# Second mixers off GpSimd, later transposes, reordered norm steps, and wider weight splits in a two-block transformer kernel

## The chip, the cores and the metric

The kernel runs on one core of a Trainium2 chip. The metric is device time of one execution, in microseconds (us). Three runs of the kernel before took 2176.16, 2175.93 and 2166.27 us, median 2175.93 us.

TensorE does matmuls and transposes, VectorE (DVE), ScalarE (ACT) and GpSimd (POOL) do the elementwise work, and SyncE (SP) issues the loads.

## The reference

The input is one sequence of 256 tokens of width 1024, float32. It goes through two layers of a first block and two of a second. Feed-forward layers have width 2816.

```python
for l in range(DEPTH):          # first block
    x = layer_norm(ALPHA * x + 0.5 * swiglu(x, ffn1_w13[l], ffn1_w2[l]), ln_g[l, 0], ln_b[l, 0])
    m = mixer(x, w_in[l], ...)  # gated recurrence (hgrn2), spatial gating unit, two branches
    x = layer_norm(ALPHA * x + m, ln_g[l, 1], ln_b[l, 1])
    x = layer_norm(ALPHA * x + 0.5 * swiglu(x, ffn2_w13[l], ffn2_w2[l]), ln_g[l, 2], ln_b[l, 2])
...
# second block, per layer: a feed-forward layer, token_mixer, a feed-forward layer,
# each between two rms_norms and added to x
qk = lax.conv_general_dilated(qk, conv_w, ...)   # in token_mixer: a filter of 5 taps along the tokens
qk = jax.nn.silu(qk + conv_b)
h_fwd = mlstm_direction(mq, mk, mv, gates[0], gates[1])   # and one backwards
merged = jnp.concatenate([attn_out, mlstm_out], axis=-1)
return merged @ w_out
```

## The kernel before

**Units and splits.** The weights come in units of 128 x 1024 floats. To keep precision, each operand is split into a high part (`hi`, written by ScalarE as a rounded copy) and a low part (`lo = w - hi`), and `mm3` does three matmuls: `x_hi w_hi`, `x_hi w_lo`, `x_lo w_hi`. In traces the parts of a weight unit are `wh` and `wl`, those of the transposed input of a layer `xh` and `xl`, those of hidden values `hT`. `split` does a unit's split. A plain unit comes from one of 4 staging buffers (`stg`) and is split in two halves of 512 columns, so that the second half's copy runs beside the first half's subtraction. `pool_share` gives every third second half of units 8 to 27 of a second mixer to GpSimd (L272).

**Products.** In the feed-forward layers some pairs of groups of columns are computed with seven products of sums of blocks in place of eight (`PRODUCTS`, `pair`). Their weight operands are blocks loaded raw (`raw`) and sums of them, which `operand` adds up on VectorE just ahead of that unit's split; a product unit is split at full width, 1024.

**Order.** The two halves of the tokens (128 each, i = 0 and 1) are two generators. Each `yield` ends a unit of TensorE work and moves a clock by one; `yield n` lets a generator or a side chain pause n clocks; `self.later(n, fn)` writes the instructions of `fn` n clocks later. From what is so written a scheduler makes the order of TensorE, VectorE and ScalarE; GpSimd and SyncE keep the written order. Each engine executes its instructions in order, so an instruction that waits holds all behind it.

**Places that the change touches.** `hidden` (L435, and the one in `pair`) finishes gate times value (`sg` L442/L445, `kp` L511) and leaves the transposes to `turn`, 2 clocks later. `ln_residual` is the first block's norm: per half h of the columns it makes `t` (L583) and its statistics, then `u` (named `t`, L592) and `x` (L593); `to_x` transposes the two `x` and writes `xh` and `xl` (L311). `sgu` is the spatial gating unit (its normed `v`, L862). In a second mixer `gates` (L1072 on) turns the gate columns `m` (L1000) with TensorE (L1080), and makes `gg`, `gc`, `Gh`, `Gl` for `mlstm`. `conv` filters `cv` into `qk`: three of four parts on VectorE, the fourth on GpSimd (L1128, L1136, L1137), and waits for it before it goes on. `rot` turns `ak` and `aq` on GpSimd and transposes 3 clocks later.

Of the kernel before, what the change touches and what calls it, by code (L numbers as in the profile page):

```python
# [11 lines left out]
F32 = mybir.dt.float32  # L12
# [35 lines left out]
ML = 2  # L48
CV = 2
CP = 2  # L50

# [3 lines left out]

OWN = 2
FFN = (("g", 8), ("s", 2, 0, 1, 2, 3), ("g", 9), ("s", 4, 16, 17, 4, 5), ("g", 10), ("s", 6, 6, 7, 18, 19),
       ("r", 8), ("r", 9), ("r", 20), ("r", 21))
# [3 lines left out]
PRODUCTS = ("p1", "p2", "q5", "p3", "p6", "p7", "q4")  # L62
LOADS = dict(p1="11", p2="21", q5="12", p3="22")
BLOCKS = ("11", "21", "12", "22")
# [14 lines left out]
class Core:  # L79
# [144 lines left out]
    def fetch(self, v):  # L224
        while self.next_dma <= min(v, self.nunit - 1):
            made = self.made[self.next_dma]
            if not self.product(self.next_dma):
                t = self.stages[self.next_dma] = self.stg.tile([P, 1024], F32, tag="stg", name=self.nm("stg"))
                for c in (slice(0, 512), slice(512, 1024)) if self.next_dma == 0 else (slice(0, 1024),):
                    self.nc.sync.dma_start(t[:, c], self.a["ws"][made][:, c])  # L230
            elif made[0] in LOADS:
                t = self.raw[made[:2]] = self.whp.tile([P, 1024], F32, tag="w", name=self.nm("raw"))
                self.nc.sync.dma_start(t, self.block(LOADS[made[0]], *made[1:]))
            self.next_dma += 1
# [3 lines left out]

    def operand(self, p, u, base):


        raw, add = self.raw, self.nc.vector.tensor_add
        if p in ("q5", "p6"):
            t = raw["p1", u]
            add(t, t, raw["q5" if p == "q5" else "p3", u])  # L245
            return t
        if p == "p7":
            t = raw.pop(("p3", u))
            add(t, t, raw.pop(("q5", u)))
            return t  # L250
        if p == "q4":
            t = raw.pop(("p1", u))
            add(t, t, raw.pop(("p2", u)))
            return t
        return raw[p, u]

    def split(self, u):
        while self.next_split <= min(u, self.nunit - 1):
            v = self.next_split
            self.fetch(v)  # L260
            made = self.made[v]
            product = self.product(v)
            w = self.operand(*made) if product else self.stages.pop(v)
            hi = self.whp.tile([P, 1024], F32R, tag="w", name=self.nm("wh"))
            lo = self.whp.tile([P, 1024], F32R, tag="w", name=self.nm("wl"))
            halves = [slice(0, 512), slice(512, 1024)]
            for h, c in enumerate([slice(0, 1024)] if product else halves):
                r = self.nc.scalar.activation(hi[:, c], w[:, c], AF.Copy)  # L268
                if v < 3:
                    self.pin(r)  # L270
                if h and self.pool_share(*self.phase[v]):
                    self.nc.gpsimd.tensor_tensor(lo[:, c], w[:, c], hi[:, c], op=ALU.subtract)  # L272
                else:
                    self.nc.vector.tensor_sub(lo[:, c], w[:, c], hi[:, c])  # L274
            self.units[v] = [hi[:, c] for c in halves], [lo[:, c] for c in halves]
            self.next_split += 1
            self.fetch(v + STAGES)

    def pool_share(self, kind, n):
        return kind == "mixer2" and 8 <= n < 28 and n % 3 == 2  # L280

# [153 lines left out]
    def hidden(self, J, i, acc, g):  # L435
# [18 lines left out]

        self.later(2, turn)

# [32 lines left out]
    def pair(self, J, g, ks):  # L489
# [20 lines left out]
        def hidden(i, t, sg):  # L510
# [7 lines left out]

            self.later(2, turn)

# [51 lines left out]
    def ln_residual(self, i, accs, l, n, pre=None):  # L572
# [9 lines left out]
        for h in range(2):  # L582
            nc.vector.scalar_tensor_tensor(t[h], self.x[i][h], ALPHA, accs[h], op0=ALU.mult, op1=ALU.add)  # L583
            nc.vector.bn_stats(st[:, 6 * h:6 * h + 6], t[h])
        mv = self.small(2)
# [3 lines left out]

        def norm(h, g, b):  # L590
            u, x = self.slot(name="t"), self.slot(name="x")
            nc.vector.scalar_tensor_tensor(u, t[h], mv[:, 0:1], g[h], op0=ALU.subtract, op1=ALU.mult)  # L592
            nc.vector.scalar_tensor_tensor(x, u, rs, b[h], op0=ALU.mult, op1=ALU.add)  # L593
            return x

        xs = [norm(h, *((gr, br) if pre else (g, b))) for h in range(2)]
        self.accs_live -= 1
# [3 lines left out]
        if pre:  # L601
            xs = [norm(h, g, b) for h in range(2)]
            rs2 = self.rsq2(self.sumsq(xs))
# [241 lines left out]
    def sgu(self, i, l, z, res):  # L845
# [16 lines left out]
        nc.vector.scalar_tensor_tensor(v, gv, rs, bb, op0=ALU.mult, op1=ALU.add)  # L862
        yield 2
        ps = self.sm()
# [7 lines left out]
        yield 2  # L872
        res["ubT"] = self.to_T(ub, "ubT")
# [90 lines left out]
    def mixer2(self, i, rs, l):  # L964
# [23 lines left out]
        def gates(k):  # L988
# [12 lines left out]
            if i == 1:  # L1001
                self.later(2, lambda: self.start(self.gates(l, J)))

# [6 lines left out]
        def rot(name, scale):  # L1010
            def f(acc):
# [20 lines left out]

                self.later(3, turn)
            return f
# [37 lines left out]
    def gates(self, l, J):  # L1072
# [12 lines left out]
        nc.vector.scalar_tensor_tensor(e, f, -1.0, f, op0=ALU.mult, op1=ALU.max)  # L1085
        yield 1
        nc.scalar.activation(e, e, AF.Exp, scale=-1.0)
        nc.scalar.activation(e, e, AF.Ln, bias=1.0)
        yield 2
        nc.vector.scalar_tensor_tensor(e, f, 0.0, e, op0=ALU.min, op1=ALU.subtract)  # L1090
# [6 lines left out]
        nc.vector.tensor_sub(g, ig, c)  # L1097
        yield 2
# [3 lines left out]
        yield 2  # L1102

# [14 lines left out]
    def conv(self, l, J, name):  # L1118
# [3 lines left out]

        def part(kt, eng, step):
            t, src = tiles[kt // 2][:, kt % 2], J[name][kt // 2][:, kt % 2]
            kk = kt + (4 if name == "mk" else 0)
            w = lambda j: self.prm[:, PRM_CW + (8 * l + kk) * 5 + j:PRM_CW + (8 * l + kk) * 5 + j + 1]
            bia = self.prm[:, PRM_CB + 8 * l + kk:PRM_CB + 8 * l + kk + 1]
            eng.tensor_scalar(t, src, w(2), bia, op0=ALU.mult, op1=ALU.add)  # L1128
            u = self.slot((P, S), name="cu") if eng is nc.gpsimd else None
            for j in (0, 1, 3, 4):  # L1130
                to = slice(max(0, 2 - j), S - max(0, j - 2))
                at = slice(max(0, j - 2), S - max(0, 2 - j))
                if u is None:
                    eng.scalar_tensor_tensor(t[:, to], src[:, at], w(j), t[:, to], op0=ALU.mult, op1=ALU.add)  # L1134
                else:
                    eng.tensor_scalar(u[:, to], src[:, at], w(j), None, op0=ALU.mult)  # L1136
                    eng.tensor_tensor(t[:, to], t[:, to], u[:, to], op=ALU.add)  # L1137
                if step:
                    yield step

        side = self.start(part(3, nc.gpsimd, CP))
        for kt in range(3):
            yield from part(kt, nc.vector, 0)
            yield CV
        while not side["done"]:
            yield 1
        ths = []
# [461 lines left out]
```

## Time and profile before

| what | value |
|---|---|
| median of three runs | 2175.93 us |
| profiled execution, its own time | 2170.28 us |
| its span | 2168.5 us |
| TensorE busy | 97%, 9904 matmuls |
| VectorE busy | 87% |
| ScalarE busy | 62% |
| GpSimd busy | 14% |
| granted TensorE clock, mean | 0.994 |

The span is from the first to the last instruction of the program. Busy shares are of this span. A row such as `PE g L286 <- DVE x L593` says that TensorE stood until VectorE's instruction of line 593 on tile `x` had ended. The granted clock is 1.00 at 2.4 GHz and 0.50 at 1.2 GHz.

### The profile page before, as it was taken

What the parts mean: (1) busy time and instruction counts of PE and PEld (TensorE: products, weight loads), DVE (VectorE), ACT (ScalarE), POOL (GpSimd) and SP (SyncE); (2) the same over time, 40 slices, a digit from 0 to 9 for tenths busy, and PEclk for the clock granted to TensorE, in tenths of its full rate; (3) what the DMA queues carried; (4) which work ended last, traced back from release to release, by engine and by line L of the source; (5) the groups of instructions that cost most, each with busy time, mean ns of one, the idle gap of its engine ahead of it and who ended that gap; (6) DMA issues with size and microseconds to landing.
All of it is one profiled execution on the core that took longest, in us unless ns stands there. A gap on an engine that the chain in (4) does not pass through costs nothing.

```text
span 2168.5 us, 28547 instructions
## 1 busy us (share of the span) xinstructions
PE 2106.6 (97%) x9904; PEld 1730.7 (80%) x9904; DVE 1878.8 (87%) x2842; ACT 1352.8 (62%) x2352; POOL 304.8 (14%) x319
## 2 busy tenths in 40 slices
PE   8999999999999999999999998999999999899998
PEld 7877888888788788888778786788878878688887
DVE  7998787899889878698989988689998998877995
ACT  6665755566566575565656664666666666576663
POOL 0000420000000033000000305610200020650000
PEclk9999999999999999999999999999999999999999
DMA  8447455455554745545555553534655546343552
GB/s 310 184 176 238 151 186 191 145 209 204 212 185 175 229 150 181 183 160 203 196 192 200 199 194 112 169 117 152 235 197 184 188 170 223 107 148 126 206 193 97
DMA packets 115296, 394.55 MB, mean 182 GB/s; under 512 B 12880, under 2 KB 15312, under 8 KB 115152
## 3 DMA queue, kind: packets, MB, share of 16 engines
q1 hardware_dynamic: 115152, 392.73, 52.4%
q8 instruction: 78, 1.28, 0.2%
q14 instruction: 66, 0.54, 0.1%
HBM read 391.63 MB, written 1.05 MB: 181 GB/s over the span
## 4 chain that ended last, share of the span: by engine, by line
PE 74%; DVE 13%; DMA 4%; issue 3%; ACT 3%; POOL 2%; SPq 0%; DVEq 0%; POOLq 0%; ACTq 0%
PE g L302 30%; PE big L302 21%; PE g L547 16%; DVE wl L274 7%; DMA stg<-in_ws_dram 4%; PE g L286 4%; ACT wh L268 2%; PE big L1263 1%; DVE raw L245 1%; PE big L1292 1%; DVE qk L1134 1%; PE big L792 1%; POOL qk L1128 1%; DVE kp L504 0%; DVE x L593 0%
## 5 line engine op out<-in xcount | busy, mean ns | idle before, releaser
L274 DVE TENSOR_TENSOR wl<-stg,wh 128x512 fp32r<-128x512 f32 x1026 | 691.1, 707 | 126.5 <-ACT wh L268 119.4
L268 ACT ACTIVATE wh<-stg 128x512 fp32r<-128x512 f32 x1040 | 601.0, 624 | 200.8 <-DMA stg<-in_ws_dram 77.9
L302 PE MATMUL g<-wh,xh 128*128 128x512 f32 x1184 | 482.2, 407 | 9.1 <-ACT wh L268 6.0
L302 PE MATMUL g<-wl,xh 128*128 128x512 f32 x1184 | 467.7, 395 | 14.2 <-POOL wl L272 13.5
L302 PE MATMUL g<-wh,xl 128*128 128x512 f32 x1184 | 464.4, 394 | 0.0
L268 ACT ACTIVATE wh<-raw 128x1024 fp32r<-128x1024 f32 x336 | 349.4, 1056 | 175.5 <-DVE raw L245 51.0
L274 DVE TENSOR_TENSOR wl<-raw,wh 128x1024 fp32r<-128x1024 f32 x336 | 409.5, 1234 | 25.1 <-ACT wh L268 23.2
L302 PEld LDWEIGHTS g<-wl,xh 128*128 128x128 f32 x1184 | 225.5, 190 | 57.3 <-POOL wl L272 14.3
L302 PEld LDWEIGHTS g<-wh,xh 128*128 128x128 f32 x1184 | 225.1, 190 | 57.1 <-ACT xh L310 6.8
L302 PEld LDWEIGHTS g<-wh,xl 128*128 128x128 f32 x1184 | 224.4, 190 | 50.2 <-DVE xl L311 2.0
L302 PE MATMUL big<-wh,hT 128*128 128x512 f32 x640 | 183.3, 390 | 0.0
L547 PE MATMUL g<-wl,Xh 128*128 128x512 f32 x384 | 150.8, 393 | 0.0
L547 PE MATMUL g<-wh,Xl 128*128 128x512 f32 x384 | 150.3, 391 | 0.0
L547 PE MATMUL g<-wh,Xh 128*128 128x512 f32 x384 | 149.6, 390 | 0.0
L302 PEld LDWEIGHTS big<-wh,hT 128*128 128x128 f32 x640 | 120.1, 188 | 25.3
L410 POOL TENSOR_TENSOR m<-m,nhalf 128x1 f32<-128x1 f32 (+1 forms) x24 | 22.6, 940 | 792.8 <-DVE m L409 792.8
L302 PE MATMUL big<-wh,hTh 128*128 128x512 f32 x384 | 124.9, 392 | 0.0
L302 PE MATMUL big<-wl,hTh 128*128 128x512 f32 x384 | 124.3, 390 | 0.0
L302 PE MATMUL big<-wh,hTl 128*128 128x512 f32 x384 | 124.0, 390 | 0.0
L245 DVE TENSOR_TENSOR raw<-raw,raw 128x1024 f32<-128x1024 f32 x96 | 120.6, 1267 | 1.9 <-DMA raw<-in_ws_dram 1.4
L547 PE MATMUL g<-wh,xh 128*128 128x512 f32 x288 | 114.6, 398 | 1.4 <-ACT kp L501 1.4
L547 PE MATMUL g<-wl,xh 128*128 128x512 f32 x288 | 112.5, 390 | 0.0
(325 smaller groups left out, 3227.9 us busy)
## 6 DMA issues: line engine op xcount, KB each, us to landing
stg<-in_ws_dram SPq DMA_DIRECT2D x519, 512.0 KB, 4.4
raw<-in_ws_dram SPq DMA_DIRECT2D x192, 512.0 KB, 5.2
row<-in_norm_gain_dram SPq DMA_DIRECT2D x24, 256.0 KB, 6.7
row<-in_ln_g_dram SPq DMA_DIRECT2D x12, 256.0 KB, 4.9
row<-in_ln_b_dram SPq DMA_DIRECT2D x12, 256.0 KB, 6.2
xT<-in_xT_dram SPq DMA_DIRECT2D x4, 256.0 KB, 6.0
x<-in_x_dram SPq DMA_DIRECT2D x4, 256.0 KB, 9.1
out_dram<-x SPq DMA_DIRECT2D x4, 256.0 KB, 2.0
```

Source lines behind the costliest of these rows:

```text
L245: add(t, t, raw["q5" if p == "q5" else "p3", u])
L268: r = self.nc.scalar.activation(hi[:, c], w[:, c], AF.Copy)
L274: self.nc.vector.tensor_sub(lo[:, c], w[:, c], hi[:, c])
L286: self.nc.tensor.transpose(tp[:, hs(j)], src[:, hs(j)], self.ident)
L302: self.nc.tensor.matmul(accs[c], a, b[c], start=start and q == 0, stop=stop and q == 2)
L410: self.nc.gpsimd.tensor_tensor(out, out, self.nhalf[:, 0:n], op=ALU.pow)
L547: nc.tensor.matmul(bank[p], x[:, hs(k)], w[j], start=first[p] == p and k + q == 0, stop=k == 3 and q == 2, skip_group_check=True)
L792: nc.tensor.matmul(ps[:, 64 * h:64 * h + 64].rearrange("p (c m) -> p c m", m=m), Z[:, hs(h)], view(Z[:, hs(h)], m)[:, :, 1, :], start=True ...
L1128: eng.tensor_scalar(t, src, w(2), bia, op0=ALU.mult, op1=ALU.add)
L1134: eng.scalar_tensor_tensor(t[:, to], src[:, at], w(j), t[:, to], op0=ALU.mult, op1=ALU.add)
L1263: nc.tensor.matmul(ps[:, hh * S + j * P:hh * S + j * P + P], J["aq", i][r, hs(head // 2)], J["ak", j][r, hs(head // 2)], start=True, stop= ...
L1292: nc.tensor.matmul(o[:, 64 * hh:64 * hh + 64], pT[:, hs(2 * hh + j)], J["av", j][:, head * 64:head * 64 + 64], start=j == 0, stop=j == 1)
```

## The change

The second mixers' weight halves all go to VectorE, and the filter's fourth part too; the first multiply of each filter part goes to ScalarE. Transposes of hidden values are written 4 clocks later in place of 2, others and the gates' and gating unit's steps 1 to 4 clocks later than before. In the norm both halves of each step stand together. A sum of weight blocks is written right behind the split of the unit ahead of it. Plain units of feed-forward layers, from the ninth unit of the program on, are split at full width like the products.

```diff
-CV = 2
-CP = 2
+CV = 3
...
+TURNS = 4
...
-            w = self.operand(*made) if product else self.stages.pop(v)
+            w = self.raw[made] if product else self.stages.pop(v)
...
-            for h, c in enumerate([slice(0, 1024)] if product else halves):
+            wide = v >= 8 and self.phase[v][0] == "ffn"
+            for h, c in enumerate([slice(0, 1024)] if wide else halves):
                 r = self.nc.scalar.activation(hi[:, c], w[:, c], AF.Copy)
...
-                if h and self.pool_share(*self.phase[v]):
-                    self.nc.gpsimd.tensor_tensor(lo[:, c], w[:, c], hi[:, c], op=ALU.subtract)
-                else:
-                    self.nc.vector.tensor_sub(lo[:, c], w[:, c], hi[:, c])
+                self.nc.vector.tensor_sub(lo[:, c], w[:, c], hi[:, c])
...
             self.fetch(v + STAGES)
+            if self.next_split < self.nunit and self.product(v + 1):
+                self.sum(*self.made[v + 1])
...
-        self.later(2, turn)
+        self.later(TURNS, turn)
...
         for h in range(2):
             nc.vector.scalar_tensor_tensor(t[h], self.x[i][h], ALPHA, accs[h], op0=ALU.mult, op1=ALU.add)
+        for h in range(2):
             nc.vector.bn_stats(st[:, 6 * h:6 * h + 6], t[h])
...
+        def norm(g, b):
+            u, x = ([self.slot(name=n) for _ in range(2)] for n in "tx")
+            for h in range(2):
+                nc.vector.scalar_tensor_tensor(u[h], t[h], mv[:, 0:1], g[h], op0=ALU.subtract, op1=ALU.mult)
+            for h in range(2):
+                nc.vector.scalar_tensor_tensor(x[h], u[h], rs, b[h], op0=ALU.mult, op1=ALU.add)
             return x
...
-                self.later(2, lambda: self.start(self.gates(l, J)))
+                self.later(4, lambda: self.start(self.gates(l, J)))
...
-                self.later(3, turn)
+                self.later(5, turn)
...
-            eng.tensor_scalar(t, src, w(2), bia, op0=ALU.mult, op1=ALU.add)
+            nc.scalar.activation(t, src, AF.Identity, scale=w(2), bias=bia)
             for j in (0, 1, 3, 4):
...
+                nc.vector.scalar_tensor_tensor(t[:, to], src[:, at], w(j), t[:, to], op0=ALU.mult, op1=ALU.add)
+
+        for kt in range(4):
+            part(kt)
             yield CV
```

In `sgu` two pauses grow from 2 to 4 and to 3 clocks; in `gates` four pauses grow from 1, 2, 2, 2 to 2, 3, 3, 6. VectorE has 642 fewer 512-wide and 328 more 1024-wide subtractions of plain weights, 12 fewer multiplies and 16 more steps of the filter; ScalarE 656 fewer 512-wide and 328 more 1024-wide copies and 16 more filter steps; GpSimd 50 fewer instructions. TensorE and SyncE have the same instructions as before, and SyncE's stand in the same order.

The order changes as follows at three places. First GpSimd in the first second mixer, around the filter and the turn of `ak`; `wl` is a weight half, `qk` and `cu` belong to the filter, `rw` and `ak` to the turn, `vx` is a small constant, `m` a norm factor. Before:

```order
L272 TENSOR_TENSOR wl_12286<-stg_12156,wh_12285 128x512
L1136 TENSOR_SCALAR cu_12210<-cv_12037,prm 128x254
L1137 TENSOR_TENSOR qk_12208<-qk_12208,cu_12210 128x254
L1128 TENSOR_SCALAR qk_12367<-cv_12147,prm 128x256
L1136 TENSOR_SCALAR cu_12369<-cv_12147,prm 128x254
L1137 TENSOR_TENSOR qk_12367<-qk_12367,cu_12369 128x254
L1136 TENSOR_SCALAR cu_12369<-cv_12147,prm 128x255
L1137 TENSOR_TENSOR qk_12367<-qk_12367,cu_12369 128x255
L272 TENSOR_TENSOR wl_12414<-stg_12257,wh_12413 128x512
L1020 TENSOR_TENSOR rw_12442<-ak_12440,con 128x64
```

and now:

```order
L620 TENSOR_TENSOR m_11687<-m_11687,nhalf 128x1
L1007 MEMSET vx_11865 128x4x4
L1021 TENSOR_TENSOR rw_12012<-ak_12010,con 128x64
L1022 TENSOR_TENSOR rw_12012<-ak_12010,con 128x64
L1023 TENSOR_TENSOR rw_12012<-ak_12010,con 128x64
L1024 TENSOR_TENSOR rw_12012<-ak_12010,con 128x64
```

The filter steps and the weight halves are gone; the turn of `ak` follows the small steps directly.

Second TensorE in the first layer's second feed-forward layer, between the last product of a pair (`g_5553` before, `g_5376` now) and the transposes of its `kp`; `g_5850`, `g_5851`, `g_5658` and `g_5659` are the next group of columns. Before:

```order
L547 MATMUL g_5553<-wh_5729,xl 128x512
L302 MATMUL g_5850<-wh_5791,xh 128x512
...
L302 MATMUL g_5851<-wh_5791,xl 128x512
L286 MATMUL g_5864<-con,kp_1366_5776 128x128 x4
L302 MATMUL g_5850<-wh_5805,xh 128x512
```

and now:

```order
L545 MATMUL g_5376<-wh_5545,xl 128x512
L300 MATMUL g_5658<-wh_5607,xh 128x512
...
L300 MATMUL g_5659<-wh_5619,xl 128x512
L284 MATMUL g_5684<-con,kp_1366_5592 128x128 x4
L300 MATMUL g_5658<-wh_5625,xh 128x512
```

Between the product's last matmul and the transposes stood 12 matmuls, those of one unit of both halves of the tokens; now there are 24.

Third VectorE in the norm behind the same layer, first half of the tokens; `t`, `x` and `xl` are as above, `wl` are weight units of the next layer. Before:

```order
L586 BN_AGGR m_5135<-m_5128 128x2
L274 TENSOR_TENSOR wl_5256<-stg_5126,wh_5255 128x512
L409 TENSOR_SCALAR m_5137<-m_5135 128x1
L592 SCALAR_TENSOR_TENSOR t_5140<-t_5129,m_5135,row_4105 128x512
L274 TENSOR_TENSOR wl_5298<-stg_5154,wh_5297 128x512
L593 SCALAR_TENSOR_TENSOR x_5141<-t_5140,m_5137,row_4109 128x512
L592 SCALAR_TENSOR_TENSOR t_5144<-t_5130,m_5135,row_4107 128x512
L274 TENSOR_TENSOR wl_5298<-stg_5154,wh_5297 128x512
L593 SCALAR_TENSOR_TENSOR x_5145<-t_5144,m_5137,row_4111 128x512
L274 TENSOR_TENSOR wl_5330<-stg_5168,wh_5329 128x512
L311 TENSOR_TENSOR xl<-g_5194,xh 128x512
```

and now:

```order
L585 BN_AGGR m_4975<-m_4968 128x2
L407 TENSOR_SCALAR m_4977<-m_4975 128x1
L592 SCALAR_TENSOR_TENSOR t_4980<-t_4969,m_4975,row_3996 128x512
L592 SCALAR_TENSOR_TENSOR t_4981<-t_4970,m_4975,row_3998 128x512
L594 SCALAR_TENSOR_TENSOR x_4982<-t_4980,m_4977,row_4000 128x512
L594 SCALAR_TENSOR_TENSOR x_4983<-t_4981,m_4977,row_4002 128x512
L273 TENSOR_TENSOR wl_5090<-stg_4966,wh_5089 128x1024
L273 TENSOR_TENSOR wl_5124<-stg_4992,wh_5123 128x1024
L273 TENSOR_TENSOR wl_5160<-stg_5004,wh_5159 128x1024
L309 TENSOR_TENSOR xl<-g_5030,xh 128x512
```

The weight work that stood between the norm's steps has moved, part of it ahead of them and three whole units between the second `x` and the first `xl`.

## Rows read from the trace of the kernel before

**Rows 1.** The page's busy time, share of the span and instructions of each engine.
```profile
PE 2106.6 (97%) x9904; PEld 1730.7 (80%) x9904; DVE 1878.8 (87%) x2842; ACT 1352.8 (62%) x2352; POOL 304.8 (14%) x319
```
**Rows 2.** TensorE's waits: engine and line, waited for: total us, times, longest.
```profile
PE g L302 <- POOL wl L272: 13.5, 2, 6.8
PE g L286 <- DVE x L593: 10.5, 9, 2.3
PE g L286 <- DVE kp L511: 6.9, 6, 1.6
...
PE g L286 <- DVE sg L445: 4.7, 7, 1.0
PE big L1080 <- DVE m L1000: 3.2, 2, 1.6
...
PE big L866 <- DVE v L862: 2.2, 2, 1.2
...
PE g L302 <- DVE wl L274: 0.7, 1, 0.7
```
**Rows 3.** GpSimd in time, one second mixer: start, us, what [idle before].
```profile
1340.25 6.70 POOL L1128 TENSOR_SCALAR qk<-cv,prm 128x256 f32<-128x256 f32 x1 [6.66 <-DVE cv L980]
...
1352.91 2.29 POOL L272 TENSOR_TENSOR wl<-stg,wh 128x512 fp32r<-128x512 f32 x1
```
**Rows 4.** Windows: stretch, length, busy us (instructions) by engine, granted clock, DMA share, GB/s.
```profile
1290.00:1348.00 58.00, 55.84 (x281) 46.36 (x280) 50.96 (x97) 32.27 (x60) 22.73 (x19) 1.00 0.38 132
1355.20:1360.70 5.50, 5.45 (x15) 4.12 (x16) 0.96 (x2) 1.55 (x3) 5.16 (x10) 0.50 0.30 95
1360.70:1366.00 5.30, 5.30 (x29) 4.13 (x27) 4.69 (x6) 3.39 (x7) 3.75 (x3) 1.00 0.12 25
1881.00:1886.30 5.30, 5.30 (x14) 4.00 (x15) 0.77 (x2) 1.42 (x3) 4.96 (x10) 0.50 0.28 99
```
**Rows 5.** Groups by line and form, whole run: busy us, mean ns, idle before.
```profile
L274 DVE TENSOR_TENSOR wl<-stg,wh 128x512 fp32r<-128x512 f32 x1026 | 691.1, 707 | 126.5 <-ACT wh L268 119.4 <-PE g L286 2.8 <-PE g L302 2.3
L268 ACT ACTIVATE wh<-stg 128x512 fp32r<-128x512 f32 x1040 | 601.0, 624 | 200.8 <-DMA stg<-in_ws_dram 77.9 <-PE g L302 71.7 <-PE big L302 42.7
...
L268 ACT ACTIVATE wh<-raw 128x1024 fp32r<-128x1024 f32 x336 | 349.4, 1056 | 175.5 <-DVE raw L245 51.0 <-DVE raw L253 47.7 <-DVE raw L249 24.8
...
L1134 DVE SCALAR_TENSOR_TENSOR qk<-cv,prm,qk 128x255 f32<-128x255 f32 x24 | 14.2, 628 | 0.0
```
**Rows 6.** TensorE and VectorE in time, around one pair's transposes.
```profile
1210.94 0.39 PE L547 MATMUL g<-wl,Xh 128*128 128x512 f32 x1
1211.17 0.39 PE L547 MATMUL g<-wh,Xl 128*128 128x512 f32 x1
...
1215.93 0.68 DVE L511 SCALAR_TENSOR_TENSOR kp<-kp,kp 128x512 f32<-128x512 f32 x1
...
1216.75 0.63 PE L286 MATMUL g<-con,kp 128*128 128x128 f32 x4 [1.57 <-DVE kp L511]
```
**Rows 7.** TensorE and VectorE in time, around the norm shown in the order.
```profile
557.12 0.66 PE L286 MATMUL g<-con,x 128*128 128x128 f32 x4 [0.63 <-DVE x L593]
...
558.25 0.75 DVE L593 SCALAR_TENSOR_TENSOR x<-t,m,row 128x512 f32<-128x512 f32 x1
...
559.14 0.63 PE L286 MATMUL g<-con,x 128*128 128x128 f32 x4 [1.36 <-DVE x L593]
...
559.51 0.69 DVE L311 TENSOR_TENSOR xl<-g,xh 128x512 fp32r<-128x512 f32 x1
```
**Rows 8.** VectorE in time: two half units, and two wide ones, in a row.
```profile
605.41 1.29 DVE L274 TENSOR_TENSOR wl<-stg,wh 128x512 fp32r<-128x512 f32 x2
607.75 2.36 DVE L274 TENSOR_TENSOR wl<-raw,wh 128x1024 fp32r<-128x1024 f32 x2
```
**Rows 9.** SyncE's waits ahead of its loads: total us, times, longest.
```profile
SPq L230 <- DVE wl L274: 1239.8, 381, 19.6
```

More of the change, by code (lines that the diff above doesn't have):

```diff
@@ L62 @@
 PRODUCTS = ("p1", "p2", "q5", "p3", "p6", "p7", "q4")
-LOADS = dict(p1="11", p2="21", q5="12", p3="22")
+LOADS = dict(p1=("11", "p1"), p2=("21", "p2"), q5=("12", "12"), p3=("22", "p3"))
 BLOCKS = ("11", "21", "12", "22")
@@ L231, in fetch @@
             elif made[0] in LOADS:
-                t = self.raw[made[:2]] = self.whp.tile([P, 1024], F32, tag="w", name=self.nm("raw"))
-                self.nc.sync.dma_start(t, self.block(LOADS[made[0]], *made[1:]))
+                t = self.raw[LOADS[made[0]][1], made[1], made[2]] = self.whp.tile([P, 1024], F32, tag="w", name=self.nm("raw"))
+                self.nc.sync.dma_start(t, self.block(LOADS[made[0]][0], *made[1:]))
             self.next_dma += 1
@@ L237, in block, with sum, add @@
         return self.a["ws"][base + 2 * BLOCKS.index(b) + u]
[L239 to L255, printed above, removed]
+    def sum(self, p, u, base):
+        raw = self.raw
+        def add(t, other):
+            self.nc.vector.tensor_add(t, t, other)
+            raw[p, u, base] = t
+        if p == "q5":
+            add(raw.pop(("p1", u, base)), raw["12", u, base])
+        elif p == "p6":
+            add(raw.pop(("q5", u, base)), raw["p3", u, base])
+        elif p == "p7":
+            add(raw.pop(("p3", u, base)), raw.pop(("12", u, base)))
+        elif p == "q4":
+            add(raw.pop(("p6", u, base)), raw.pop(("p2", u, base)))
     def split(self, u):
@@ L277, in split @@
             self.fetch(v + STAGES)
-    def pool_share(self, kind, n):
-        return kind == "mixer2" and 8 <= n < 28 and n % 3 == 2
+            if self.next_split < self.nunit and self.product(v + 1):
+                self.sum(*self.made[v + 1])
     def transposed(self, src, n=4):
@@ L517, in turn @@
                     J["h", i, 2 * g + c] = hi[:, hs(c)], lo[:, hs(c)]
-            self.later(2, turn)
+            self.later(TURNS, turn)
         def after(p):
@@ L588, in ln_residual @@
         self.rsqrt(rs, mv[:, 1:2], LN_EPS)
[L590 to L593, printed above, removed]
+        def norm(g, b):
[4 more added lines that the diff above has]
+                nc.vector.scalar_tensor_tensor(x[h], u[h], rs, b[h], op0=ALU.mult, op1=ALU.add)
             return x
-        xs = [norm(h, *((gr, br) if pre else (g, b))) for h in range(2)]
+        xs = norm(*((gr, br) if pre else (g, b)))
         self.accs_live -= 1
@@ L601, in ln_residual @@
         if pre:
-            xs = [norm(h, g, b) for h in range(2)]
+            xs = norm(g, b)
             rs2 = self.rsq2(self.sumsq(xs))
@@ L862, in sgu @@
         nc.vector.scalar_tensor_tensor(v, gv, rs, bb, op0=ALU.mult, op1=ALU.add)
-        yield 2
+        yield 4
         ps = self.sm()
@@ L871, in sgu @@
                                            z["u"][:, hs(h)], op0=ALU.add, op1=ALU.mult)
-        yield 2
+        yield 3
         res["ubT"] = self.to_T(ub, "ubT")
@@ L1085, in gates @@
         nc.vector.scalar_tensor_tensor(e, f, -1.0, f, op0=ALU.mult, op1=ALU.max)
-        yield 1
+        yield 2
         nc.scalar.activation(e, e, AF.Exp, scale=-1.0)
         nc.scalar.activation(e, e, AF.Ln, bias=1.0)
-        yield 2
+        yield 3
         nc.vector.scalar_tensor_tensor(e, f, 0.0, e, op0=ALU.min, op1=ALU.subtract)
@@ L1097, in gates @@
         nc.vector.tensor_sub(g, ig, c)
-        yield 2
+        yield 3
         for r in turn:
@@ L1101, in gates @@
         nc.vector.tensor_add(c, c, G)
-        yield 2
+        yield 6
         ps = self.sm()
@@ L1121, in conv, with part @@
         tiles = [self.slot((P, 2, S), name="qk") for _ in range(2)]
-        def part(kt, eng, step):
+        def part(kt):
             t, src = tiles[kt // 2][:, kt % 2], J[name][kt // 2][:, kt % 2]
@@ L1127, in part @@
             bia = self.prm[:, PRM_CB + 8 * l + kk:PRM_CB + 8 * l + kk + 1]
-            eng.tensor_scalar(t, src, w(2), bia, op0=ALU.mult, op1=ALU.add)
-            u = self.slot((P, S), name="cu") if eng is nc.gpsimd else None
+            nc.scalar.activation(t, src, AF.Identity, scale=w(2), bias=bia)
             for j in (0, 1, 3, 4):
@@ L1132, in part @@
                 at = slice(max(0, j - 2), S - max(0, 2 - j))
[L1133 to L1143, printed above, removed]
+                nc.vector.scalar_tensor_tensor(t[:, to], src[:, at], w(j), t[:, to], op0=ALU.mult, op1=ALU.add)
+        for kt in range(4):
+            part(kt)
             yield CV
-        while not side["done"]:
-            yield 1
         ths = []
```

## The prediction
> **What bounds the kernel now.** I read the page's shares first: TensorE is busy for 97% of a span of 2168.5 us [rows 1]. It does the same 9904 matmuls in both kernels, so a change can only take away time in which it stands still or runs slowly. I therefore read next the list of what it waited for [rows 2]. Weights made on VectorE are late once, by 0.7 us. Weights made on GpSimd are late twice, by 13.5 us together. The rest are short waits in front of transposes, for the last VectorE step of a chain: `kp` and `sg` (hidden values of the feed-forward layers), `x` (the norm), `m` (the gate columns of the second mixer), `v` (the first mixer). So the weights are far enough ahead, and what ends last are short chains queued on VectorE among weight work, plus GpSimd in two places.
>
> **Weights off GpSimd.** GpSimd runs in written order. In each second mixer a filter step took 6.70 us there and others followed, so a `wl` half queued behind them ended at 1355.2 [rows 3]; TensorE stood for half of the 13.5 us here and half in the other layer. After both stalls its granted clock is 0.50, the 1.2 GHz level: 15 matmuls in 5.5 us, then 29 in 5.3 us at full clock [rows 4]. At the later rate 15 take 2.7 us, so 2.8 us are lost; by the same rate 14 in 5.3 us lose 2.7 us. Taking these GpSimd steps away gives 13.5 + 5.5 = 19.0 us. What comes to VectorE: 14 halves of 0.707 us [rows 5], 9.9 us, and 16 more filter steps of at most 0.628 us, 10.0 us, less the 12 multiplies that go to ScalarE: at most 20 us over two layers. Before the stall VectorE is busy 50.96 of 58 us [rows 4] and no weights are late, so I cost it at nothing. The end where that fails is rival 2.
>
> **Later transposes.** With `TURNS` 4 the transposes stand two units (12 matmuls) later behind their chain, as the order rows on TensorE show. One matmul follows another by 0.23 us [rows 6], so they come 2.7 us later. The longest wait is 1.6 us for `kp` and 1.0 for `sg` [rows 2], and the example [rows 6] waits 1.57 us. All are covered: 6.9 + 4.7 = 11.6 us. The lower end is half of it, if wide weight steps lengthen these chains. The values are used many units later, so the delay itself costs nothing. The `yield`s in the gates and in the gating unit do the same for `m` (3.2) and `v` (2.2): 5.4 us, with longest waits of 1.6 and 1.2 us against at least one more unit (1.4 us).
>
> The same numbers have a price. The gate chain and the filters now start the second mixer's recurrent part (`mlstm`) later, so one of its stages lies among the attention steps, and the transposes of the cells stand between the last rows of the mixer instead of among attention. No row shows what this costs. From below it is nothing. From above it is two transposes with their evacuations in each of two layers, each some 1.5 us by the steps around the norm [rows 7]: 6 us. I take 3 us, the middle, since half the transposes keep other matmuls around them.
>
> **The norm.** This is the part whose gain I do not believe. Today TensorE waits 10.5 us for `x` [rows 2], all in the norms of the first block, as at 557.12 (0.63) and 559.14 (1.36) [rows 7]. The new order puts the two `x` next to each other, ahead of the weight work. But TensorE then needs `xl`, the low part of the transposed `x`, also from VectorE. The order rows show three 1024-wide `wl` between the second `x` and the first `xl`, where one 512-wide half stood. VectorE runs in order. Counted in units, 233.5 stood before that `xl` and 234 stand there now; the steps of the chain are the same. A wide one follows another after 2.36 - 1.22 = 1.14 us [rows 8], a half after 0.61 [rows 8], so the half unit more is 0.6 us and three or four wide ones give back 0.08 each. The end of the first `xl`, 559.51 + 0.69 = 560.2 [rows 7], stays within half a microsecond. TensorE, which today reaches its third matmul behind the transposes at about 560.3 (559.14 + 0.63, then two matmuls, by estimate), finds `xl` there at the same time as before. The wait moves from `x` to `xl`, about one for one: 0 us. The ends are +10.5 (no wait on `xl`) and -6 (half a unit, 0.6 us, at some ten norms).
>
> Perfetto Trace Analysis of the Trainium skill (Optimizing Scalar/DVE Operations) says that where these engines are not saturated and still leave bubbles elsewhere, smaller instructions let work end sooner, which speaks against the wide splits. By that rule the norms would come out at the lower end, -6 us, by rows 7 and 8. The trace so far agrees in part, with a VectorE that TensorE waits for often and briefly.
>
> **Wide splits and sums ahead.** 328 plain units become one copy and one subtraction. VectorE saves 0.08 us a unit by rows 8, 26 us in all, and ScalarE 2 x 0.624 - 1.056 = 0.19 us by its means [rows 5], 63 us. The sums keep their count and move one unit forward. Weights are not what TensorE waits for (0.7 us), so I put 0 on the path; relief for the chains could make it a few us.
>
> **Sum.** 19.0 + 11.6 + 5.4 - 3 + 0 = 33 us. The profiled execution took 2170.3 us (span 2168.5 and 1.8 around it); the three runs are 2166.3, 2175.9 and 2176.2, so their median lies above it. The mean of the four is 2172.2; I take the sum from there, rounded up by 1 us to 34 for the relief of the last part: 2138 us.
>
> **Rivals.**
> 1. The norm pays too: `xl` is not late because VectorE arrives there ahead of time, relieved by the wide splits. For it speaks that VectorE idles often for ScalarE's halves (119 us [rows 5]); against it, the order. 2138 - 10.5 - 1.5 = 2126 us.
> 2. The second mixers give their stall back: up to 20 us of VectorE work come into stretches where it is busy 88% [rows 4], and gates, filters and weights queue on one engine. For it speaks that `m` is late there already (3.2 us); against it, that no VectorE weights are late. 2138 + 19 = 2157 us, and with the norms' lower end 2163 to 2165.
> 3. The change doesn't do what it says: transposes moved away still wait because ScalarE and VectorE hold wide pieces, and the removed GpSimd wait appears as one on VectorE's weights. 2170 us.
> 4. Slower: the staging buffers become the bound. SyncE's weight loads wait for the subtraction that frees a buffer, 381 times, 1239.8 us [rows 9]. Two halves overlap ScalarE and VectorE: 0.62 + 1.29 = 1.91 us to the end of the unit; a wide one takes 1.06 + 1.22 = 2.28, so each buffer is held 0.37 us longer. Over 328 units that is 121 us if nothing hides it and 30 us if four buffers share it. It decides from the point at which TensorE begins to wait on VectorE's weights, now 0.7 us; to end slower it must cost over 45 us. Half of the full price, 60 us: 2198 us. Against it: the loads wait because the buffers ahead are full, not the other way.
>
> **How the numbers follow.** Forecast 0.57, with its own range 2126 to 2150; rival 1 0.18; rival 2 0.11; rival 3 0.08; rival 4 0.06. About 0.5%, 11 us, is what a measurement can tell here, so faster means below 2165 and slower above 2187. Faster: 0.57 + 0.18 + most of 0.11 = 0.84; same: 0.10; slower: 0.06. Low end: rival 1 with the 3 us of the mixers not paid and some relief more, and its scatter of runs, 2117. High end: rival 2 with half of the norms' loss, 2161. Outside lie rivals 3 and 4 and the edges.
>
> **What would show it.** Right: no wait of TensorE on GpSimd `wl`, `kp` and `sg` nearly gone, full clock in both second mixers, waits of several us on `xl` or on ScalarE's `xh` behind the norms and few on `x`; TensorE's idle time down by about 27 us. Wrong: waits on VectorE's `wl`, a low clock at new places, or TensorE standing in the tail of the mixers for `mT` or in their middle for `gc` or `Gl`.

## The result, and the profile after

The changed kernel takes 2151.02 us, median of 4 runs (2150.62 to 2151.26), against 2174.00 for the kernel before in the same session (4 runs, 2166.27 to 2176.16): a ratio of 0.9906, 95% interval 0.9889 to 0.9923. By the ratio it is 20 us faster, by the medians 23. The prediction said 2138 us: its direction was right, and some two thirds of its gain of 34 us came. The time lies inside its whole range, 2117 to 2161, and 1 us outside the 2126 to 2150 of its own forecast. Most of its terms, taken one by one, were wrong all the same. That they cancelled as far as they did is luck, and the experiments show how it came about.

The page's busy row after, for [rows 1]:

```profile
PE 2103.2 (98%) x9904; PEld 1730.3 (80%) x9904; DVE 1849.6 (86%) x2532; ACT 1329.9 (62%) x2040; POOL 248.3 (12%) x269
```

TensorE's waits after, for [rows 2]: engine and line, waited for: total us, times, longest.

```profile
PE g L284 <- POOL aq L1026: 6.6, 2, 3.3
...
PE g L284 <- DVE kp L509: 5.1, 3, 2.1
PE g L284 <- DVE sg L443: 4.6, 3, 1.9
...
PE big L300 <- DVE A L797: 2.6, 2, 1.3
PE big L793 <- DVE E L777: 1.9, 4, 0.5
PE g L284 <- DVE x L594: 1.9, 1, 1.9
PE g L284 <- DVE sg L440: 1.7, 2, 0.9
...
PE big L300 <- DVE mTl L293: 1.1, 2, 0.5
...
PE g L300 <- DVE xl L309: 0.7, 2, 0.5
```

All waits of this list sum to 54.8 us before and 39.2 after, 15.6 less. TensorE's busy time falls by 2106.6 - 2103.2 = 3.4 us. Together that is the 19.0 us by which the span shrank (2168.5 to 2149.5); the medians differ by more because the runs before scatter. The list shows what the prediction did not have: the weights' wait on GpSimd is gone, but `aq`, which nobody waited for, now costs 6.6 us; `x` is nearly gone and `xl` did not replace it; `kp` and `sg` are nearly as they were; `m` and `v` are gone and `A`, `E` and `mTl` stand there instead.

GpSimd in time in the second mixer of [rows 3], after: start, us, what [idle before]. Below it VectorE in the same stretch.

```profile
1340.82 5.87 POOL L1021 TENSOR_TENSOR rw<-aq,con 128x64 f32<-128x64 f32 x1 [9.15 <-ACT aq L1014]
...
1348.97 0.32 POOL L1026 TENSOR_TENSOR aq<-rw 128x64 f32<-128x64 f32 x1
```

```profile
1341.62 1.88 DVE L273 TENSOR_TENSOR wl<-stg,wh 128x512 fp32r<-128x512 f32 x3
1343.43 1.27 DVE L1145 SCALAR_TENSOR_TENSOR qk<-th,qk 128x512 f32<-128x512 f32 x2
1344.63 1.88 DVE L273 TENSOR_TENSOR wl<-stg,wh 128x512 fp32r<-128x512 f32 x3
1346.87 0.68 DVE L1116 TENSOR_TENSOR Gl<-gG,Gh 4x512 fp32r<-4x512 f32 x1 [0.36 <-ACT Gh L1115]
```

A step of 0.32 us took 5.87: it ended at 1346.69, right after VectorE, busy without a break until 1346.51, paused for 0.36 us. The filter step of 6.70 us in [rows 3] stood at the same place, 1340.25. In two kernels of the experiments a step of `ak`'s turn is held up in this stretch, for 4.35 us (later transposes alone) and 3.39 us (mixers alone). In the one with `aq`'s turn on VectorE no GpSimd step starts there before 1345.44, and the first takes 1.57 us. So the delay belongs to the place and not to the filter: the GpSimd steps that come there are held up, whatever they are.

The clock around both `aq` waits (columns as in [rows 4]):

```profile
1349.30:1352.80 3.50, 3.46 (x10) 2.29 (x10) 0.00 (x0) 1.20 (x3) 1.69 (x6) 0.61 0.19 76
1352.80:1356.30 3.50, 3.50 (x16) 2.46 (x15) 1.98 (x4) 2.97 (x8) 1.73 (x3) 1.00 0.25 90
...
1873.20:1881.50 8.30, 8.30 (x20) 5.46 (x19) 3.33 (x6) 5.52 (x12) 2.73 (x7) 0.52 0.27 80
1881.50:1886.00 4.50, 4.50 (x22) 3.62 (x22) 3.20 (x6) 2.62 (x6) 0.00 (x0) 1.00 1.01 290
```

Near the 1.2 GHz level (0.52) 20 matmuls take 8.3 us; at the rate of the next row they would take 20 x 4.5 / 22 = 4.1, by estimate. In the first layer 10 in 3.5 us lose 3.5 - 10 x 3.5 / 16 = 1.3 us. The loss is 5.5 us in all, as much as before the change.

### The profile page after: what moved, and what is told of

Its sections match the earlier page's. It is cut to its first block, busy times and chain, and to the rows that moved or that the text cites. A ratio compares the mean times of both kernels' runs of the same rounds, so it can differ in the third digit from the quotient of the medians.

```text
span 2149.5 us, 27945 instructions
## 1 busy us (share of the span) xinstructions
PE 2103.2 (98%) x9904; PEld 1730.3 (80%) x9904; DVE 1849.6 (86%) x2532; ACT 1329.9 (62%) x2040; POOL 248.3 (12%) x269
## 4 chain that ended last, share of the span: by engine, by line
PE 81%; DVE 5%; issue 2%; ACT 2%; POOL 1%; DVEq 0%; POOLq 0%; ACTq 0%
PE g L300 32%; PE big L300 24%; PE g L545 18%; PE g L284 3%; DVE wl L273 2%; PE big L1254 1%; PE big L1283 1%; POOL rw L1021 1%; DVE raw L246 0%; ACT wh L270 0%; ACT xh L308 0%; PE big L1167 0%; PE big L1201 0%; PE big L793 0%; PE big L1173 0%
## 5 line engine op out<-in xcount | busy, mean ns | idle before, releaser
L273 DVE TENSOR_TENSOR wl<-stg,wh 128x512 fp32r<-128x512 f32 (+1 forms) x712 | 666.3, 957 | 122.6 <-ACT wh L270 114.1
L270 ACT ACTIVATE wh<-stg 128x512 fp32r<-128x512 f32 (+1 forms) x712 | 565.0, 823 | 222.2 <-DMA stg<-in_ws_dram 82.1
L273 DVE TENSOR_TENSOR wl<-raw,wh 128x1024 fp32r<-128x1024 f32 x336 | 415.6, 1251 | 28.4 <-ACT wh L270 26.2
L246 DVE TENSOR_TENSOR raw<-raw,raw 128x1024 f32<-128x1024 f32 x192 | 233.0, 1231 | 5.5 <-DMA raw<-in_ws_dram 5.0
```

What stands on the lines that cost most here:

```text
L246: self.nc.vector.tensor_add(t, t, other)
```

## The experiments

Four kernels put one part alone into the kernel before. Its median in that session is 2169.49 us.

**Mixers alone.**

```diff
-                if h and self.pool_share(*self.phase[v]):
-                    self.nc.gpsimd.tensor_tensor(lo[:, c], w[:, c], hi[:, c], op=ALU.subtract)
...
+            nc.scalar.activation(t, src, AF.Identity, scale=w(2), bias=bia)
```

> The kernel before with one part alone: the second mixers' weight halves and the filter's fourth part off GpSimd (the filter's first multiply on ScalarE); transposes, norm, splits and sums as before. Theory 1 (the prediction's term A): both waits on GpSimd's weights go (13.5 us) and the full clock stays there (5.5 us): 19 us faster. Theory 2 (the stretched GpSimd step only changes its owner): GpSimd's next first step in that place is the rotary turn of aq; it stands behind VectorE's unbroken weight work as the filter step did, and aq's transposes come two units earlier than in the changed kernel. TensorE then waits for aq at least 3.3 us in each layer, up to 6, with half clock behind it: 2 to 8 us faster only.

Measured: 2172.73 us, ratio 1.0018 (1.0007 to 1.0029), 3 to 4 us slower. TensorE's waits in it:

```profile
PE g L282 <- POOL ak L1021: 16.6, 4, 7.8
...
PE g L282 <- POOL aq L1021: 3.3, 2, 1.7
```

The 13.5 us of weights came back as 19.9 us of `ak` and `aq`, whose turns GpSimd does. Theory 2 is right in kind: the delay only changed its owner. But the owner is mostly `ak` (16.6) and not `aq` (3.3), and in place of a gain of 2 to 8 us there is a small loss.

**Later transposes alone.**

```diff
-        self.later(2, turn)
+        self.later(TURNS, turn)
...
-                self.later(3, turn)
+                self.later(5, turn)
```

> The kernel before with one part alone: TURNS 4 and all the later yields of gates, rotary and gating unit. Theory 1 (the prediction's terms B, C and D): waits on kp, sg, m and v all go, 17 us, less 3 in the mixers' tails: 14 us faster. Theory 2 (the two-clock delay moves the transposes of the second pair value of a product and of sg by 12 matmuls, but those of the first pair value, which are due while a row unit is counted twice, by 2): four of the kp waits stay, 4 to 5 us; 8 to 10 us faster, and the GpSimd weight waits as before.

Measured: 2165.84 us, ratio 0.9984 (0.9975 to 0.9994). The waits:

```profile
PE g L286 <- POOL ak L1025: 13.5, 2, 6.8
PE g L286 <- DVE sg L445: 6.7, 3, 2.6
...
PE g L286 <- DVE kp L511: 3.7, 4, 1.3
PE g L286 <- DVE x L593: 3.1, 4, 1.4
PE g L286 <- DVE sg L442: 3.0, 2, 2.4
PE big L302 <- DVE A L796: 2.6, 2, 1.3
...
PE big L792 <- DVE E L776: 1.9, 4, 0.5
```

It gained 4 us, less than either theory. The stall of 13.5 us on GpSimd changed its owner here too, from `wl` to `ak`. Half of `kp` stays, as theory 2 said; `sg` grew from 5.5 to 9.7 us, which no theory said; and `A` and `E` of the first mixers are new, so they come from this part. `x` fell here by itself.

**The norm alone.**

```diff
+        for h in range(2):
             nc.vector.bn_stats(st[:, 6 * h:6 * h + 6], t[h])
...
-        xs = [norm(h, *((gr, br) if pre else (g, b))) for h in range(2)]
+        xs = norm(*((gr, br) if pre else (g, b)))
```

> The kernel before with one part alone: the norm's steps in pairs. Theory 1 (the prediction's term E): the wait moves from x to xl one for one, 10 us on xl and xh behind the norms, time within 2 us of before. Theory 2 (xl is in time because the two x end sooner by one whole step): waits on x fall from 10.5 to about 2 us, xl stays under 1: 7 to 9 us faster.

Measured: 2165.50 us, ratio 0.9985 (0.9974 to 0.9996).

```profile
PE g L302 <- DVE xl L311: 3.7, 6, 1.1
...
PE g L286 <- DVE x L596: 2.1, 3, 0.9
```

Between the two theories: `x` gives 8.4 us, `xl` takes 3.7.

**Wide splits alone.**

```diff
+            wide = product or v >= 8 and self.phase[v][0] == "ffn"
+            for h, c in enumerate([slice(0, 1024)] if wide else halves):
```

> The kernel before with one part alone: plain units of the feed-forward layers split at full width. Theory 1 (the prediction's term F): nothing on the path, within 2 us, VectorE's busy time down by some 25 us, ScalarE's by some 60. Theory 2 (a 1024-wide subtraction in front of a chain's step holds it twice as long): waits on kp, sg and x rise together by 2 to 6 us, and so does the time. Theory 3 (staging buffers become the bound): waits on VectorE's weights appear, tens of us.

Measured: 2176.00 us, ratio 1.0028 (1.0018 to 1.0038), slower. VectorE's busy time fell by 16.8 us and ScalarE's by 29.6. `x` fell from 10.5 to 5.8 us. These waits grew or are new:

```profile
PE g L287 <- DVE kp L512: 7.8, 5, 2.5
...
PE g L287 <- POOL ak L1026: 4.4, 2, 2.2
PE g L303 <- DVE xl L312: 4.0, 5, 1.2
```

Theory 2 is right about the time, 6.5 us, and not about the waits: of the three that it named `kp` rose, by 0.9, and `x` and `sg` fell. All waits add up to 56.9 us against 54.8 before, so its trace places only a third of the 6.5 us. Theory 3 fails: no wait on VectorE's weights.

The four parts alone add up to +3.2 - 3.7 - 4.0 + 6.5 = +2 us. The sums written ahead were not run alone. So the gain lies in the parts' company or in those sums.

**Two parts together.** The diff is that of the first two experiments.

> The kernel before with two parts together: the second mixers off GpSimd and the later transposes; norm, splits and sums as before. Alone they gave +4 and -3.5 us. Theory 1 (they only pay together: with the work off GpSimd its first step is stretched once and not several times, and two more units cover most of it): waits on GpSimd ak and aq fall to 6 to 9 us, no wait on weights: 2152 to 2158 us. Theory 2 (they add up): 2168 to 2172 us, and the gain of the whole is in the sums ahead.

Measured: 2159.98 us against 2172.84, ratio 0.9939 (0.9925 to 0.9954). The waits:

```profile
PE g L282 <- DVE sg L441: 6.8, 3, 2.6
PE g L282 <- POOL aq L1021: 6.6, 2, 3.3
PE g L282 <- DVE x L589: 5.1, 4, 2.8
```

13 us, where alone the parts lost 3 and gained 4. The waits on `ak` and `aq`, 19.9 us with the mixers alone, are down to 6.6. Without weights and filter GpSimd has only its turns to do there, and the turns' transposes stand five clocks behind them in place of three, which covers all but 3.3 us in each layer. That it is these clocks and not the gates' is argued: no run moves the turns' transposes by themselves. Theory 1 is right in kind, the time 2 us above its range.

**Everything but the splits and sums.**

```diff
-            wide = v >= 8 and self.phase[v][0] == "ffn"
+            wide = product
...
-            if self.next_split < self.nunit and self.product(v + 1):
-                self.sum(*self.made[v + 1])
```

> The changed kernel without its last part: plain units split in halves and the sums right ahead of their own split, as before; mixers, transposes and norm changed. Theory 1 (the prediction's term F, nothing on the path): 2149 to 2153 us. Theory 2 (the part costs what wide splits alone cost, 6 us): 2143 to 2147 us. Theory 3 (it pays in company, since the chains behind the later transposes get the VectorE time it frees): 2154 to 2160 us, with more waiting for x, xl and sg.

Measured: 2158.24 us against 2169.88, ratio 0.9943 (0.9920 to 0.9965). By the ratios the splits and sums are worth (0.9943 - 0.9906) x 2170 = 8 us in company (the far ends of the two intervals leave -1 to 16), the time of theory 3. Its trace has 41.8 us of waits against 39.2, with `sg` at 10.4 in place of 6.3 and `kp` shorter; `x` and `xl`, which theory 3 named too, are not longer. Its mean granted clock is 0.993 against 0.996. So a third of it is in the waits and the rest in TensorE's busy time (2107.3 against 2103.2), which the lower clock fits. How much of the 8 us is the sums' and how much the wide splits', no run tells.

This kernel is also the two parts together plus the norm's new order.

```profile
PE g L282 <- DVE x L592: 1.1, 1, 1.1
```

The norm's order takes `x` from 5.1 to 1.1 us and leaves `xl` at 0.5. In the time no gain of it is seen: the ratios are 0.9943 with it and 0.9939 without.

**The turn of `aq` on VectorE.**

```diff
-                g = nc.gpsimd
+                g = nc.vector if name == "aq" else nc.gpsimd
```

> The changed kernel with the rotary turn of aq on VectorE in place of GpSimd (six 128x64 steps in each of four turns). Theory 1 (GpSimd's first step stands behind VectorE's unbroken work, and TensorE behind it): the wait on aq, 6.6 us, goes, and with it the half clock behind it, about 5 us more: 2138 to 2142 us. Rival (the place only changes owner again, since VectorE is as full there): a wait of 2 to 3 us on VectorE's aq or on ak comes in each layer, the half clock stays: 2147 to 2152 us.

Measured: 2141.72 us, ratio 0.9859 (0.9845 to 0.9874), 9.3 us below the changed kernel. Its waits are 6.8 us less in sum, and TensorE's busy time is 2099.1 us against 2103.2. No wait is left between 1338 and 1376 or between 1860 and 1905 us, and the clock is full there:

```profile
1345.00:1350.00 5.00, 5.00 (x28) 3.76 (x29) 4.17 (x8) 4.45 (x12) 4.48 (x7) 1.00 0.65 216
...
1865.00:1875.00 10.00, 10.00 (x46) 7.32 (x46) 9.01 (x16) 9.00 (x21) 6.60 (x9) 1.00 0.77 248
```

Theory 1 is right.

**The first pair value's transposes later.**

```diff
-            self.later(TURNS, turn)
+            self.later(TURNS if i else TURNS + 3, turn)
```

> The changed kernel with the transposes of the first hidden value of each pair 3 clocks later (7 in place of 4), which in the written order is 18 matmuls, 4.1 us. Theory 1 (the wait on kp stayed because four clocks moved these transposes by 2 matmuls only): the three waits, 5.1 us, go: 2144 to 2147 us. Rival (VectorE is full in these stretches, so that the chain's end moves with the transposes, or the next step is late instead): the wait turns up at kp's second value, at sg or at VectorE's weights, 2149 to 2153 us.

Measured: 2152.60 us, ratio 0.9906 (0.9893 to 0.9919), no gain: the rival in kind, at a place that it had not named. The wait on `kp` did go, and this came:

```profile
PE g L545 <- DVE hT L449: 4.6, 4, 2.4
```

TensorE now waits at the next product for VectorE's last step on an earlier transpose. VectorE is full ahead of these waits: 7.87 of the 7.90 us before the longest, 7.07 of 7.10 and 7.47 of 7.50 before the next two. Moving one step only makes the next one late.

**The gating unit's pauses.** On top of `aq` on VectorE:

```diff
-        yield 4
+        yield 3
         ps = self.sm()
...
-        yield 3
+        yield 2
         res["ubT"] = self.to_T(ub, "ubT")
```

> The changed kernel with aq's turn on VectorE (2141.7 us by itself) and the gating unit's pauses at 3 and 2 in place of 4 and 3. Theory 1 (the later pauses took the wait on v away and put waits on A, 2.6 us, and E, 1.9 us, of the recurrence in its place; one unit more than before covers v): A and E go, v stays away: 2136 to 2139 us. Rival (A and E wait for VectorE's weights, not for the gating unit's place): 2141 to 2144 us, with v back at up to 2.2 us.

Measured: 2138.23 us, ratio 0.9850 (0.9829 to 0.9871), the lowest median here, though by the ratios (0.9859 without this step) the two kernels are not apart. In the waits theory 1 holds: `A` at L797 and `E` are gone, 4.5 us, `v` stays away, and `ub`, new with 2.3 us, takes half of it back.

**A probe of GpSimd beside VectorE**, in three forms. The stream is VectorE's, `fn` one of three kinds; the four GpSimd steps read `q`, which ScalarE writes:

```python
for _ in range(n):
    fn(t["ob"], t["a"])
for k in range(4):
    nc.gpsimd.tensor_tensor(w, q, t["b"][:, 0:64], op=ALU.subtract)
```

> A probe that leaves out the whole computation and writes sums of its input: four GpSimd subtractions of 128x64 each time, released by ScalarE at the start of a stream of VectorE instructions of 128x512: none, 4 or 12 additions with both inputs in SBUF, 12 additions with one input in PSUM, 12 multiply-adds with a single SBUF input. Theory 1 (GpSimd gets in only when VectorE leaves a gap, where VectorE reads two SBUF inputs): the first GpSimd step takes 0.3 us with no stream, about 2 us with 4, about 7 us with 12, and 0.3 us with one input in PSUM. Theory 2 (the first step after a pause is slow by itself): the same time in every trial. Theory 3 (the two share evenly): about 0.6 us in all trials with a stream.

> The probe again, with the stream's instructions writing four tiles in turn, so that no VectorE instruction waits for the one before it (in the first probe they started every 0.72 us at a length of 0.69, a gap each time, and GpSimd's four steps took 2.5 us against 1.5 with no stream, whatever the stream's length). Theory 1 (GpSimd gets in only in gaps of a VectorE that reads two SBUF inputs): the stream of 12 runs at 0.60 us each without a gap, and GpSimd's first step takes as long as the rest of it, 6 to 7 us, about 2 us with 4; with one input in PSUM 0.4 us. Theory 2 (each GpSimd step waits for one VectorE instruction at most): four steps take 2.5 us whatever the stream.

In the first form four steps took 1.51 us with no stream, 2.53 and 2.52 with 4 and 12 additions, 1.52 beside PSUM inputs. The stream's length did not matter, so theory 1 of this form fails; and with no stream four steps take 1.51 us after a pause of 5.8 us, so a first step is not slow by itself (theory 2). GpSimd in the second form, in the order no stream, 4, 12, PSUM, single input:

```profile
6.55 1.51 POOL L48 TENSOR_TENSOR w<-q,b 128x64 f32<-128x64 f32 x4 [6.11 <-ACT q L44]
9.51 2.52 POOL L48 TENSOR_TENSOR w<-q,b 128x64 f32<-128x64 f32 x4 [1.45 <-ACT q L44]
13.48 2.52 POOL L48 TENSOR_TENSOR w<-q,b 128x64 f32<-128x64 f32 x4 [1.44 <-ACT q L44]
22.28 1.51 POOL L48 TENSOR_TENSOR w<-q,b 128x64 f32<-128x64 f32 x4 [6.28 <-ACT q L44]
30.29 1.79 POOL L48 TENSOR_TENSOR w<-q,b 128x64 f32<-128x64 f32 x4 [6.50 <-ACT q L44]
```

Theory 2 of the second form holds. For the third form:

```diff
+            if delay:
+                nc.scalar.activation(z[:, 0:delay], t["oa"][:, 0:delay], AF.Copy)
```

> The probe a third time: always 12 VectorE additions of 128x512, two GpSimd steps of 128x64, and nine delays before GpSimd's release (ScalarE copies none or 64 to 512 columns first), so that its first step comes at different points of a VectorE instruction; first with all inputs in SBUF, then with the eighth addition reading PSUM. In the probe before, the step always came 0.09 us ahead of the next addition. Theory 1 (GpSimd wins only if it is there when the port changes hands, and otherwise stays out as long as VectorE goes on with two SBUF inputs without a gap; this is what made 0.32 us steps last 5.9 us in the whole kernel): at most delays the first step takes 3 to 7 us, to the end of the stream, and in the second set ends at the eighth addition; at some it takes under 1 us. Theory 2 (it waits for one VectorE instruction at most at any point): under 1.1 us at every delay, and the 5.9 us steps of the whole kernel have another reason, which stays open.

The two steps together, with the longest and the shortest time of all delays in both sets:

```profile
15.63 1.53 POOL L47 TENSOR_TENSOR w<-q,b 128x64 f32<-128x64 f32 x2 [7.64 <-ACT q L43]
...
84.01 1.07 POOL L47 TENSOR_TENSOR w<-q,b 128x64 f32<-128x64 f32 x2 [6.89 <-ACT q L43]
```

No delay holds GpSimd longer than about one VectorE instruction. SBUF — State Buffer of the Trainium skill (Who interferes with whom) says that VectorE with two SBUF inputs contends with GpSimd's reads, and with at most one, outside its two-port modes, does not. The probe agrees for additions: 1.51 us beside PSUM inputs and 2.52 beside two SBUF inputs. Beside the multiply-adds, which have one SBUF input, it was 1.79 us, and they lasted 0.54 us in place of 0.41; whether they ran in a two-port mode no run here shows. But the contention of the probe does not make 0.32 us into 5.87. In the changed kernel both long `aq` steps end at a pause of VectorE; in the kernel with later transposes the step of 4.35 us ends during a filter step of VectorE, with no pause. The probe's stream had one kind of instruction at a time, the kernel's a mix of filter steps, scans and weights. What keeps GpSimd out there stays open.

## Why the prediction came out as it did

**Weights off GpSimd, 19.0 us.** Right about the weights, wrong about the stall. The sentence that failed is "Taking these GpSimd steps away gives 13.5 + 5.5". The 13.5 us went, 6.6 came back as the wait for `aq`, and the 5.5 us of low clock stayed whole, behind `aq`. The term paid about 7 us; of the 12 left, moving `aq`'s turn gained 9.3 afterwards. The prediction asked what VectorE would do with the work that came to it (nothing was late for it), and not which step of GpSimd would stand first in the same place. The order rows of GpSimd had it: behind the removed rows comes `rw<-ak`, the turn. The mixers alone show it: with three clocks behind the turns, the stall stays whole.

**Later transposes, 11.6 us.** This is the term that failed outright: `kp` gave 1.8 us, `sg` lost 0.8. "With `TURNS` 4 the transposes stand two units (12 matmuls) later" holds for the second value of each pair: 12 matmuls stood between its last product and its transposes, and 24 stand there now. It does not hold for the first value: most of its transposes stood 13 to 23 matmuls behind and stand 18 to 22 behind now; at the three that still wait, 16, 17 and 17 became 21, 18 and 18. The program's clock explains it. Behind a second value come units of 12 matmuls that move the clock by two, once in `both` and once by their `yield`. Behind a first value comes one such unit (`on`) and then units of a product, 6 matmuls for one clock, so that two more clocks are worth 6 matmuls as written. The order rows shown were of a second value, but the example of [rows 6] is a first one, and so were four of the six waits.

The remaining waits come from what is ahead in the queues. ScalarE, then VectorE, then TensorE, around one of them after:

```profile
1537.10 1.06 ACT L270 ACTIVATE wh<-raw 128x1024 fp32r<-128x1024 f32 x1 [6.36 <-DVE raw L246]
1538.07 0.58 ACT L499 ACTIVATE kp<-g 128x512 f32<-128x512 f32 x1
```

```profile
1539.34 0.68 DVE L502 TENSOR_TENSOR kp<-kp,g 128x512 f32<-128x512 f32 x1
1539.93 1.22 DVE L273 TENSOR_TENSOR wl<-stg,wh 128x1024 fp32r<-128x1024 f32 x1
1541.07 0.69 DVE L509 SCALAR_TENSOR_TENSOR kp<-kp,kp 128x512 f32<-128x512 f32 x1
```

```profile
1541.90 0.63 PE L284 MATMUL g<-con,kp 128*128 128x128 f32 x4 [1.53 <-DVE kp L509]
```

ScalarE stands 6.36 us for a sum on VectorE, and `kp`'s first step stands behind the copy that waits. The two longest `sg` waits (1.9 us each) have the same shape: a copy waits 3.1 us for a sum, and the activation of `sg` is behind it. The delay is made on ScalarE by a wait for VectorE, before the chain begins, and a chain counted from its VectorE steps does not show it. That this wait is what makes the chain late is read from these traces; no run took it away.

**Gates and gating unit, 5.4 us, less 3 for the tails.** `m` and `v` went as said, 5.4 us. `A`, `E` and `mTl` took 5.6. The price was sought in the second mixers' tails (`mTl`, 1.1) and lay mostly in the first mixers, at `A` and `E`, with the gating unit's own pauses; the kernel with one clock less showed that. Net nothing, in place of 2.4. The 3 us for the tails came from no row, as the prediction says itself; what shows there is `mTl`.

**The norm, 0 us.** Wrong the other way: `x` went from 10.5 to 1.9 and `xl` only came to 0.7, 7.9 us; ScalarE's copies of the transposed `x` (`A`, L314) took back 1.6. VectorE, then TensorE, after, at the norm of [rows 7]:

```profile
550.98 1.41 DVE L594 SCALAR_TENSOR_TENSOR x<-t,m,row 128x512 f32<-128x512 f32 x2
552.31 3.49 DVE L273 TENSOR_TENSOR wl<-stg,wh 128x1024 fp32r<-128x1024 f32 x3
555.76 1.29 DVE L309 TENSOR_TENSOR xl<-g,xh 128x512 fp32r<-128x512 f32 x2
```

```profile
554.50 1.03 PE L284 MATMUL g<-con,x 128*128 128x128 f32 x8
```

Both `x` are ready at 552.4 and TensorE turns them at 554.5 without a wait: VectorE is ahead of it by 2.1 us, so the three wide pieces before `xl` fit in between. The step that failed is "The wait moves from `x` to `xl`, about one for one": the prediction counted pieces on VectorE and left TensorE's time where it was. (It also took the first matmul that reads `xl` for the third behind the transposes; before it is the fifth, at 560.54.) What came is what rival 1 forecast, at 0.18, but not for its reason, the relief by the wide splits: without them `x` and `xl` are as short, 1.1 and 0.5. Nor is the 7.9 us the new order's own. Alone it does 4.7 of it, the later transposes alone bring `x` to 3.1, and on top of mixers and transposes the order shows no gain in time. The rule of Perfetto Trace Analysis of the Trainium skill (Optimizing Scalar/DVE Operations) that the prediction quotes, by which wide pieces would make the norms late, is borne out by the wide splits alone (`xl` at 4.0) and not by the whole.

**Splits and sums, 0 us.** Alone the splits cost 6.5 us, in company with the sums they give some 8. They freed less than was reckoned: alone 16.8 us on VectorE and 29.6 on ScalarE, where the prediction has 26 and 63. Rival 4 is out: SyncE waited no longer for staging buffers than before (1239.8 us [rows 9]), and TensorE never for VectorE's weights.

```profile
SPq L231 <- DVE wl L273: 1227.6, 369, 14.4
```


So the sum of 33 was to be made of 19, 11.6, 2.4 and 0; by the two lists of waits it was made of 6.9 at the GpSimd weights and turns, 1.0 at `kp` and `sg`, about 0 at gates and gating unit, 7.9 at the norm, and 3.4 in TensorE's busy time; smaller waits, both ways, cancel. This list says where TensorE stood, not which part of the change earned it. The forecast of TensorE's idle time, 27 us less, met 15.6. Of the signs that the prediction named for being right, the end of the wait on GpSimd's `wl` came and `x` became short; `kp` and `sg` nearly gone, full clock in both second mixers and waits of several us on `xl` did not.

## What to carry to other kernels

When a stall behind a slow instruction is to go, ask whether the instruction or its place is slow, and which one comes first in that place afterwards. A delay written in clocks of a program should be counted in instructions at each kind of site, not at one example. Parts that alone lost 3 us and gained 4 were worth 13 us together, so that neither the sum of single parts nor their first verdicts say what a whole change does.

## What was not expected of the hardware

A GpSimd step of 0.32 us lasted 5.87 us beside a busy VectorE, once in each second mixer, with a granted clock of 0.61 and 0.52 behind it, and the same kind of step beside the probe's stream never waited for more than about one VectorE instruction. VectorE pays too: its 128x512 addition lasted 0.81 us with a GpSimd step in between and 0.68 without. With both of VectorE's inputs in SBUF the two engines disturbed each other; with one input in PSUM neither was slower; with a single SBUF input both were, GpSimd by less (1.79 us for four steps against 2.52).
